# Row sums of one probability tile in four on PoolE in a dilated-attention block

## The chip, the core and the metric

The kernel runs on one core of a Trainium2 chip. The core has a matrix engine (TensorE, PE in the profile, with its weight loads shown apart as PEld), VectorE (DVE), ScalarE (ACT), PoolE (POOL, also GpSimd) and SyncE (SP), which here only issues DMA transfers. Each engine takes its instructions in order, and they wait for each other through semaphores. The metric is the device time of one execution in microseconds, median of several runs.

## The reference

One decoder block on x of 2048 positions by 1024 features, float32. Only the attention matters here:

```python
DILATION_GROUPS = ((128, 1), (512, 4), (2048, 16))   # (window, dilation), 8 heads of 64 in each group
...
s = jnp.einsum('brnqhd,brnkhd->brnhqk', qb, kw) * (Dh ** -0.5)
s = jnp.where(valid[None, None, :, None], s, NEG_INF)      # a causal band, 128 queries by 256 keys
m = jnp.max(s, axis=-1, keepdims=True)
p = jnp.exp(s - m)
l = jnp.sum(p, axis=-1, keepdims=True)
o = jnp.einsum('brnhqk,brnkhd->brnqhd', p, vw)
...
wts = jax.nn.softmax(jnp.stack(lses, axis=0), axis=0)      # lse = m + log(l): the three groups are mixed by it
attn = jnp.sum(wts[..., None] * jnp.stack(outs, axis=0), axis=0)
```

Before it stands one input projection (queries, keys, values, gates), beside it a gated recurrence over positions (its result is `h` below, its output projection `yb`), and behind it the output projections and a layer norm. The row sum `l` is what the change computes in another way.

## The kernel before

The kernel has four stages. **A**, to about 1445 us, is the input projection with the rotary embedding and the recurrence; its results go to scratch tensors in DRAM. **B**, attention, runs to about 1645. **C** is the `yb` products, 32 jobs of 24 matmuls, in whose shadow the three attention groups are combined (`weigh`, `spread`, `combine`). **D** is the remaining projections and the norm.

Stage B is a loop over 48 rounds `i`. Four rounds (`q` = 0 to 3) make a unit `u`, which is one pair of heads of one group; units take the groups in the order 0, 2, 1, and again, for four pairs of heads. A round has four blocks `j` of 128 queries and two heads `h`, so eight score tiles. A score tile has 256 keys, or 128 where there is no block before it: `first(i, j)` is then 128. That holds for all of group 2, for all blocks of the first round of a unit of group 1, and for block 0 in the first round of a unit of group 0. I call such tiles and rounds narrow.

The work of a round is written out by hand and spread over three rounds, so that the engines run side by side:

- `scores(i)`: 24 matmuls into two PSUM tiles for each half round (tag `s`).
- `peak(i, j, h)` on VectorE: adds the mask, writes the tile to SBUF as `p` and takes the row extreme into `sta`. The tile `p` of a block comes from a pool of eight buffers, four of which are used in a round.
- `expo(i, j, h)` on ScalarE, in place on `p`: the Exp, with the row sum as accumulator output into `sta`. In the profile this is two instructions, ACTIVATE and ACTIVATION_READ_ACCUMULATOR (L1023).
- `turn(i-1, w)` on TensorE: transposes the `p` tiles of half a round into PSUM.
- `bring(i-1 or i-2, w, k, engine)`: copies these to SBUF (`ptb`), on VectorE (L1049) or ScalarE (L1047). In each round VectorE has two of the four copies for good; a third, `bring(i-2, 1, 0)`, is VectorE's if `light` is true and ScalarE's if not; the fourth, `bring(i-1, 0, 0)`, is VectorE's if `more` is true.
- `values(i-2)` on TensorE, and `leave(i-3)` on VectorE: the product with V, and its copy out of PSUM.

`leave` also queues the stores of the round (`o_scr`), and for the last pair of heads the store of the statistics `sta` to `st_scr`; they are issued on SP a round later. Stage C reads them back (`load_stats`).

Queries, keys and values of unit u + 2 are loaded from round 4u on (`unit_parts`, `loads`, two pieces a round). The keys of a unit come in two halves, `k_part(0)` and `k_part(1)`; each is cut into two pieces of 512 columns, and each piece is split into a rounded part and its remainder (`split`, lines L809 and L811: a cast and a subtraction). For the first unit ScalarE and VectorE do that, for the others PoolE. `later(lag, fn)` puts a function on a list; `run(late)`, at the start of a round, issues what has become due. From round 40 on the weights `wl` of stage C (`prep_wl`) and the first block of `h` (`load_h`) are loaded, and PoolE splits them too, two rounds later (L1100, L1103): two pieces of weights or of `h` in each of the rounds 42 to 47, and two pairs of weights after the loop.

Of the kernel before, what the change touches and what calls it, by code (L numbers as in the profile page):

```python
# [8 lines left out]
F32 = mybir.dt.float32  # L9
F32R = mybir.dt.float32r  # L10
AF = mybir.ActivationFunctionType
ALU = mybir.AluOpType
# [3 lines left out]
P = 128  # L16
# [4 lines left out]
CH = 512  # L21
# [10 lines left out]
def hybrid_block_kernel(ctx: ExitStack, tc: tile.TileContext, a: dict, out: bass.AP):  # L32
    nc = tc.nc
    sp, act, dve, pool, pe = nc.sync, nc.scalar, nc.vector, nc.gpsimd, nc.tensor

    def flat(t):
        return t.bitcast(F32)
# [24 lines left out]
    cst = ctx.enter_context(tc.tile_pool(name="cst", bufs=1))  # L62
# [15 lines left out]
    act.dma_start(lr, a["lru_vec"])  # L78
    brh = cst.tile([P, 2, 8], F32, name="brh")
    HALF = (slice(0, 64), slice(64, P))  # L80
    gr_free = [cst.tile([P, P], F32, name=f"gr{j}") for j in range(2)]
    sp2 = cst.tile([P, 8], F32, name="sp2")


# [2 lines left out]
    def big(slot, shape, dt, name):  # L87
        return (Y if slot[0] == "Y" else Z if slot[0] == "Z" else X).tile(shape, dt, name=name, tag=slot)
# [5 lines left out]
    def later(lag, fn):  # L94
        late.append((now["n"] + lag, fn))
# [4 lines left out]
    def run(queue):  # L100
        due = [x for x in queue if x[0] <= now["n"]]
        queue[:] = [x for x in queue if x[0] > now["n"]]
        for _, fn in due:
            fn()
# [443 lines left out]
    light = [("v", FT_V + 2 * j, FT_V + 2 * j + 1) for j in range(6)]  # L548
# [157 lines left out]
    for s, pl in enumerate(plan):  # L706
        if pl[4] == "ug" and not (pl[0] and pl[1][1][0] - FT_U in put_off):
            at(base[s] + 1, lambda i=pl[1][1][0] - FT_U: fetch_gr(i))
        if pl[0] and pl[4] == "ug":
            i = pl[1][1][0] - FT_U  # L710
# [38 lines left out]
    def bring(t, b, c):  # L749

        at(t - 3, lambda: [keep_raw(b, c, kk) for kk in K4])
        at(t, lambda: [one_block(b, kk) for kk in K4])
# [36 lines left out]
    def unit(u):  # L789

        return (0, 2, 1)[u % 3], u // 3

    def unit_parts(u):

        qs, ks = USLOT[u % 3]
        g, hp = unit(u)
        q = {n: qk_scr[n, 4 * g + hp] for n in ("qh", "ql", "k")}
        units[u] = [None, None]

        def k_part(j):  # L800
            cols = slice(j * S // 2, (j + 1) * S // 2)

            def split(t):
                K = units[u][1]
                if u == 0:
                    act.activation(K[:, 0, t], flat(K[:, 1, t]), AF.Copy)
                    eng = dve
                else:
                    pool.tensor_copy(K[:, 0, t], flat(K[:, 1, t]))  # L809
                    eng = pool  # L810
                eng.tensor_tensor(out=K[:, 1, t], in0=flat(K[:, 1, t]), in1=flat(K[:, 0, t]), op=ALU.subtract)  # L811

            def fn():
                if j == 0:
                    units[u][1] = big(ks, [P, 2, S], F32R, f"B{u}")
                sp.dma_start(flat(units[u][1][:, 1, cols]), q["k"][:, cols])
                for i in range(2):
                    c0 = (2 * j + i) * CH
                    later(3 + i if u < 2 else 1, lambda c0=c0: split(slice(c0, c0 + CH)))
            return fn  # L820

        def q_part(i, n):
            def fn():
                if i == 0:
                    units[u][0] = big(qs, [P, 2, S], F32R, f"A{u}")
                sp.dma_start(flat(units[u][0][:, i]), q[n])
            return fn

        return [k_part(0), k_part(1), q_part(0, "qh"), q_part(1, "ql")]
# [3 lines left out]
    def v_parts(g, j):  # L833
        src = v_scr[g][j]

        def part(i):
            def fn():
                if i == 0:
                    VT[g, j] = big(VSLOT[g, j], [P, 16, 256], F32, f"V{g}{j}")
                V = VT[g, j]  # L840
                if g == 0:
                    sp.dma_start(V[:, 4 * i:4 * i + 4], src[i * CH:(i + 1) * CH].rearrange("(n p) f -> p n f", p=P))
                elif g == 1:
                    sp.dma_start(V[:, 4 * i:4 * i + 4], src[i * CH:(i + 1) * CH].rearrange("(j r) f -> j r f", r=4))
                else:
                    sp.dma_start(V[:, 4 * i:4 * i + 4], src.rearrange("(i r) f -> i r f", r=16)[:, 4 * i:4 * i + 4])
            return fn

        return [part(i) for i in range(4)]
# [74 lines left out]
    first, second, third, firstv = unit_parts(0), unit_parts(1), unit_parts(2), v_parts(0, 0)  # L924
# [20 lines left out]
    n = len(where)  # L945
# [16 lines left out]
    at_p = stB.enter_context(tc.tile_pool(name="at_p", bufs=2, reuse_waits="tile"))  # L962
# [3 lines left out]
    def prev(g, n):  # L966
        if g == 0:
            return n - 1 if n >= 1 else None
        if g == 1:
            return n - 4 if n >= 4 else None  # L970
        return None

    st = {}

    sta, stg, ot = {}, {}, {}

    def first(i, j):
        u, q = divmod(i, 4)
        g, _ = unit(u)
        return 0 if prev(g, 4 * q + j) is not None else P  # L980
# [29 lines left out]
    def peak(i, j, h):  # L1010
        u, q = divmod(i, 4)
        lo = first(i, j)
        if h == 0:
            st["p", i, j] = p_p.tile([P, 2, 256], F32, tag="p", name=f"p{i}{j}")
        dve.tensor_tensor_reduce(out=st["p", i, j][:, h, lo:256], in0=st["s", i, j // 2][h][:, j % 2, lo:256],  # L1015
                                 in1=mask[:, lo:256], scale=1.0, scalar=3e38, op0=ALU.add, op1=ALU.min,
                                 accum_out=sta[u][:, 4 * q + j, h:h + 1])

    def expo(i, j, h):
        u, q = divmod(i, 4)  # L1020
        p = st["p", i, j][:, h, first(i, j):256]
        s = sta[u][:, 4 * q + j]
        act.activation(p, p, AF.Exp, scale=-1.0, bias=s[:, h:h + 1], accum_out=s[:, 2 + h:3 + h])  # L1023

    def turn(i, w):
        js = (2 * w, 2 * w + 1)
        pp = [st.pop(("p", i, j)) for j in js]
        tag = "s" if (i, w) == (NG - 1, 1) else "t"
        t = st["t", i, w] = [aps.tile([P, 2, 2, 2, 64], F32, tag=tag, name=f"pt{i}{w}{k}", bufs=4) for k in range(2)]
        for j in js:  # L1030
            for x in range(first(i, j) // P, 2):
                for h in range(2):
                    for k, r in enumerate(HALF):
                        pe.transpose(t[k][:, j % 2, x, h, :], pp[j % 2][r, h, x * P:(x + 1) * P], ident[r, r])  # L1034
# [61 lines left out]
    def split(h, l, eng=dve):  # L1096

        r = flat(l)
        if eng is pool:
            pool.tensor_copy(h, r)  # L1100
        else:
            act.activation(h, r, AF.Copy)
        eng.tensor_tensor(out=l, in0=r, in1=flat(h), op=ALU.subtract)  # L1103
# [17 lines left out]
    NG = 48  # L1121
# [4 lines left out]
    for i in range(NG):  # L1126
        u = i // 4
        turns, copied = i > 0, i > 1
        run(late)
        if i in VORD:  # L1130
            loads += v_parts(*VORD[i])
        if i % 4 == 0 and 1 <= u <= 9:
            loads += unit_parts(u + 2)
        for _ in range(2):
            if loads:
                loads.pop(0)()
        light = copied and (unit((i - 2) // 4)[0] == 2 or i % 3 == 1 or i == 2)
        scores(i)
        if i > 2 and ("o", i - 3) in st:
            leave(i - 3)  # L1140
        if copied:
            bring(i - 2, 1, 1, dve)
            if light:
                bring(i - 2, 1, 0, dve)
        if turns:
            expo(i - 1, 2, 1)
        if copied and not light:
            bring(i - 2, 1, 0, act)
        if turns:
            expo(i - 1, 3, 0)  # L1150
            expo(i - 1, 3, 1)
        peak(i, 0, 0)
        expo(i, 0, 0)
        for j, h in ((0, 1), (1, 0), (1, 1)):
            peak(i, j, h)
        if turns:
            turn(i - 1, 0)
            more = i in (1, NG - 1) or i % 4 == 0 and unit(u)[0] == 2
            bring(i - 1, 0, 0, dve if more else act)
            bring(i - 1, 0, 1, dve)  # L1160
        for j, h in ((0, 1), (1, 0), (1, 1)):
            expo(i, j, h)
        if copied:
            values(i - 2)
            if i == NG - 1:
                leave(i - 2, True)
        peak(i, 2, 0)
        peak(i, 2, 1)
        if turns:
            turn(i - 1, 1)  # L1170
        peak(i, 3, 0)
        peak(i, 3, 1)
        expo(i, 2, 0)
        if i in (40, 41):
            prep_wl(i - 40, 2)
        if 42 <= i < 46:
            load_h(0, 2 * (i - 42), 2)
            load_h(0, 2 * (i - 42) + 1, 2)
        if i in (46, 47):
            prep_wl(i - 44, 2)  # L1180
        now["n"] += 1
# [179 lines left out]
    for n in range(32):  # L1361
        c, f = divmod(n, 8)
# [229 lines left out]
```

## Time and profile before

| | us |
|---|---|
| median of 3 runs (2104.13 to 2104.58) | 2104.32 |
| the profiled execution, its own time | 2103.62 |
| its span, first to last instruction | 2101.9 |
| first and last Exp of attention, L1023 | 1445.7, 1641.7 |
| granted TensorE clock, mean | 0.999 |

A row of a timeline gives start, duration, engine, line, operation, output and inputs, shape and count; where the engine stood idle ahead of it, the idle time and what ended it stand in brackets. Durations of neighbours on one engine can overlap by some hundredths of a microsecond, so a price is read from the distance of two starts. VectorE's rows at L1015 are the peaks, eight in each round, so the first of each eight marks the start of a round: round 0 at 1444.7, round 8 at 1475.9, round 42 at 1618.3.

### The profile page before, as it was taken

The page shows a single profiled execution, that of the slowest core. Times are in us where ns is not written, and L with a number is a line of the kernel's source. Part 1 is how long each engine was busy: PE and PEld are TensorE (multiplying, and loading weights), DVE is VectorE, ACT ScalarE, POOL GpSimd, SP SyncE. Part 2 cuts the span into 40 slices and gives each one's busy share as a digit, 9 for nine tenths or more (in the row PEclk, how much of TensorE's full clock was granted, in tenths as well). Part 3 has the DMA queues.
Part 4 walks back from the last instruction along what each step waited for, and adds up shares of the span by engine and source line. Part 5 has one row for each costly group of instructions (what it writes and reads, how often), then busy time and mean ns, then how long its engine had stood idle before and what let it go on. Part 6 is the DMA issues. An engine that isn't in the chain of part 4 may idle for free.

```text
span 2101.9 us, 35814 instructions
## 1 busy us (share of the span) xinstructions
PE 2086.3 (99%) x12016; PEld 1726.9 (82%) x12016; DVE 1662.7 (79%) x3179; ACT 1116.7 (53%) x2341; POOL 493.1 (23%) x468
## 2 busy tenths in 40 slices
PE   8999999999999999999999999999999999999998
PEld 7888888888888888888888888888999888888887
DVE  8987888889988867787877888877999645576667
ACT  6455456457457565666666775766999411211100
POOL 1111111110111011231221222222545344431120
PEclk9999999999999999999999999999999999999999
DMA  8987997987997967777779778769996788864432
GB/s 271 276 261 225 274 285 216 282 283 235 278 294 242 332 208 204 231 227 220 225 254 278 254 252 266 252 219 374 355 359 236 228 296 281 298 224 160 154 105 71
DMA packets 327160, 524.69 MB, mean 250 GB/s; under 512 B 105536, under 2 KB 135232, under 8 KB 323136
## 3 DMA queue, kind: packets, MB, share of 16 engines
q1 hardware_dynamic: 307088, 489.54, 70.5%
q0 software_dynamic: 12256, 19.42, 5.5%
q10 hardware_dynamic: 7632, 13.44, 1.7%
q8 instruction: 96, 1.57, 0.3%
q14 instruction: 88, 0.72, 0.1%
HBM read 317.14 MB, written 190.45 MB: 241 GB/s over the span
## 4 chain that ended last, share of the span: by engine, by line
PE 91%; DVE 3%; DMA 3%; ACT 2%; issue 1%; SPq 0%; DVEq 0%; ACTq 0%
PE q L622 66%; PE yb L1340 3%; PE yb L1341 3%; PE z L1451 3%; PE yb L1342 3%; PE z L1450 3%; PE z L1452 3%; ACT p L1023 2%; DVE p L1015 2%; PE ya L1419 1%; PE ya L1418 1%; PE ya L1420 1%; PE g L492 1%; PE vtp L358 1%; DMA B<-k_scr 1%; DMA o_scr<-ot 1%
## 5 line engine op out<-in xcount | busy, mean ns | idle before, releaser
L622 PE MATMUL q<-xT,hS 128*128 128x512 f32 x1680 | 521.0, 391 | 0.0
L622 PE MATMUL q<-xT,l 128*128 128x512 f32 x1120 | 436.0, 389 | 0.0
L622 PE MATMUL q<-xB,hA 128*128 128x512 f32 x1248 | 388.9, 393 | 6.0 <-ACT xB L215 6.0
L622 PEld LDWEIGHTS q<-xT,hS 128*128 128x128 f32 x1680 | 312.9, 188 | 69.0 <-issue 5.5
L622 PE MATMUL q<-xB,l 128*128 128x512 f32 x904 | 352.9, 390 | 0.0
L622 PEld LDWEIGHTS q<-xB,hA 128*128 128x128 f32 x1248 | 233.8, 189 | 57.3 <-ACT xB L215 6.0
L622 PEld LDWEIGHTS q<-xT,l 128*128 128x128 f32 x1120 | 210.2, 188 | 44.1
L622 PEld LDWEIGHTS q<-xB,l 128*128 128x128 f32 x904 | 170.3, 188 | 36.0
L245 POOL DMA_DIRECT2D wS<-in_w_in_dram x70 | 61.9, 950 | 491.5 <-DMA wS<-in_w_in_dram 140.0
L622 PE MATMUL q<-xB,hS 128*128 128x512 f32 x560 | 174.0, 392 | 0.0
L1023 ACT ACTIVATE p<-p,sta 128x256 f32<-128x256 f32 (+1 forms) x384 | 172.7, 469 | 1.2 <-PE pt L1034 0.8
L622 PE MATMUL q<-xT,hA 128*128 128x512 f32 x560 | 173.0, 390 | 0.0
L269 ACT ACTIVATE hA<-wA 128x512 fp32r<-128x512 f32 x218 | 134.9, 623 | 54.4 <-DMA wA<-in_w_in_dram 24.9
L269 ACT ACTIVATE hS<-S 128x512 fp32r<-128x512 f32 x175 | 109.0, 623 | 79.3 <-DVE S L227 49.0
L227 POOL TENSOR_TENSOR S<-S,wA 128x512 f32<-128x512 f32 x35 | 45.5, 1301 | 391.8 <-DVE S L227 208.8
L622 PEld LDWEIGHTS q<-xT,hA 128*128 128x128 f32 x560 | 104.7, 188 | 23.0 <-issue 1.5
L622 PEld LDWEIGHTS q<-xB,hS 128*128 128x128 f32 x560 | 104.0, 188 | 22.4 <-issue 1.5
L1015 DVE CUSTOM_DVE_ANT_0 p<-s,mask 128x256 f32<-128x256 f32 (+1 forms) x384 | 116.4, 360 | 0.2 <-PE s L1008 0.2
L1451 PE MATMUL z<-wo,mh 128*128 128x512 f32 (+1 forms) x264 | 101.0, 383 | 0.0
L1452 PE MATMUL z<-wo,ml 128*128 128x512 f32 (+1 forms) x264 | 101.0, 383 | 0.0
L1450 PE MATMUL z<-wo,mh 128*128 128x512 f32 (+1 forms) x264 | 101.0, 383 | 0.0
L227 DVE TENSOR_TENSOR l<-wA,hA 128x512 fp32r<-128x512 f32 x113 | 79.3, 702 | 26.9 <-ACT hA L269 26.6
(204 smaller groups left out, 4257.0 us busy)
## 6 DMA issues: line engine op xcount, KB each, us to landing
wA<-in_w_in_dram SPq DMA_DIRECT2D x253, 256.0 KB, 4.7
wl_scr<-l SPq DMA_DIRECT2D x105, 512.0 KB, 5.2
l<-wl_scr SPq DMA_DIRECT2D x105, 512.0 KB, 4.6
sw<-y SPq DMA_DIRECT2D x384, 64.0 KB, 3.2
wS<-in_w_in_dram SPq DMA_DIRECT2D x70, 256.0 KB, 4.8
wS<-in_w_in_dram POOLq DMA_DIRECT2D x70, 256.0 KB, 6.3
qh_scr<-hi SPq DMA_DIRECT2D x48, 256.0 KB, 5.5
v_scr<-vs SPq DMA_DIRECT2D x48, 256.0 KB, 4.4
```

What stands on the lines that cost most here:

```text
L227: eng.tensor_tensor(out=out, in0=in0, in1=in1, op=op)
L245: pool.dma_start(t, w_part(s, x), accum_op=ALU.add)
L269: act.activation(h, r, AF.Copy)
L622: pe.matmul(bank, w[:, ks], x[:, kk, xx], start=(first and i == 0), stop=(last and i == 11))
L1015: dve.tensor_tensor_reduce(out=st["p", i, j][:, h, lo:256], in0=st["s", i, j // 2][h][:, j % 2, lo:256], in1=mask[:, lo:256], scale=1.0, s ...
L1023: act.activation(p, p, AF.Exp, scale=-1.0, bias=s[:, h:h + 1], accum_out=s[:, 2 + h:3 + h])
L1340: pe.matmul(yb, WL[f][:, 0, k], xx[:, 0], start=(k == 0), stop=False)
L1341: pe.matmul(yb, WL[f][:, 0, k], xx[:, 1], start=False, stop=False)
L1342: pe.matmul(yb, WL[f][:, 1, k], xx[:, 0], start=False, stop=(k == 7))
L1450: pe.matmul(z, mh[:, k], w[:, 0, hs], start=(k == 0), stop=False)
L1451: pe.matmul(z, mh[:, k], w[:, 1, hs], start=False, stop=False)
L1452: pe.matmul(z, ml[:, k], w[:, 0, hs], start=False, stop=(k == 7))
```

## The change

Four edits, all for stage B.

1. `expo` no longer asks for the row sum of block `j` = 0, in neither head. After the second of the two Exps it calls the new `add_up(i)`, which issues PoolE additions: the upper half of the columns onto the lower half, for both heads at once, and again until eight columns are left for each head. These stay in `rest_t`, one place for each of the four rounds of a unit. In the last round of the unit three more additions take all four places down to one column, into the same places of `sta` where the accumulator went before.
2. The scratch tile `grt` holds the sums between: it is the two 128 x 128 tiles `gr0` and `gr1` of stage A, now allocated as one.
3. The key splits that PoolE does for units 2 and later are due 3, 4, 5 and 6 rounds after the load instead of all one round after it.
4. `light` and `more` are true less often. `light` loses the rounds with `i % 3 == 1` outside group 2; `more` loses the first rounds of units of group 2. The copies concerned go from VectorE to ScalarE.

```diff
-    gr_free = [cst.tile([P, P], F32, name=f"gr{j}") for j in range(2)]
+    grt = cst.tile([P, 2, P], F32, name="grt")
+    gr_free = [grt[:, j] for j in range(2)]
...
-                    later(3 + i if u < 2 else 1, lambda c0=c0: split(slice(c0, c0 + CH)))
+                    later(3 + i if u < 2 else 3 + 2 * j + i, lambda c0=c0: split(slice(c0, c0 + CH)))
...
         s = sta[u][:, 4 * q + j]
-        act.activation(p, p, AF.Exp, scale=-1.0, bias=s[:, h:h + 1], accum_out=s[:, 2 + h:3 + h])
+        if j:
+            act.activation(p, p, AF.Exp, scale=-1.0, bias=s[:, h:h + 1], accum_out=s[:, 2 + h:3 + h])
+            return
+        act.activation(p, p, AF.Exp, scale=-1.0, bias=s[:, h:h + 1])
+        if h:
+            add_up(i)
+
+    fold_t = grt
+    rest_t = at_p.tile([P, 4, 2, 8], F32, name="rest_t", bufs=1)
+
+    def add_up(i):
+        u, q = divmod(i, 4)
+        src = st["p", i, 0][:, :, first(i, 0):256]
+        n = (256 - first(i, 0)) // 2
+        while n >= 8:
+            dst = rest_t[:, q] if n == 8 else fold_t[:, :, 0:n]
+            pool.tensor_tensor(out=dst, in0=src[:, :, 0:n], in1=src[:, :, n:2 * n], op=ALU.add)
+            src, n = dst, n // 2
+        if q < 3:
+            return
+        while n > 1:
+            pool.tensor_tensor(out=rest_t[..., 0:n], in0=rest_t[..., 0:n], in1=rest_t[..., n:2 * n], op=ALU.add)
+            n //= 2
+        sums = sta[u].rearrange("p (q j) f -> p q j f", j=4)[:, :, 0, 2:4]
+        pool.tensor_tensor(out=sums, in0=rest_t[..., 0], in1=rest_t[..., 1], op=ALU.add)
...
-        light = copied and (unit((i - 2) // 4)[0] == 2 or i % 3 == 1 or i == 2)
+        light = copied and (unit((i - 2) // 4)[0] == 2 or i == 2)
...
-            more = i in (1, NG - 1) or i % 4 == 0 and unit(u)[0] == 2
+            more = i in (1, NG - 1)
```

## The prediction

> **What bounds the kernel now.** I read the page first, then the busy time by windows over the attention stage, then the timeline of each engine there.
>
> ```profile
> span 2101.9 us, 35814 instructions
> PE 2086.3 (99%) x12016; PEld 1726.9 (82%) x12016; DVE 1662.7 (79%) x3179; ACT 1116.7 (53%) x2341; POOL 493.1 (23%) x468
> 1542.23:1591.89 49.66, 49.40 (x895) 45.09 (x892) 49.66 (x238) 49.40 (x209) 22.24 (x24) 1.00 0.85 320
> 1461.86:1645.51 183.65, 182.18 (x3267) 165.78 (x3264) 182.33 (x871) 180.76 (x767) 103.76 (x112) 1.00 0.83 306
> ```
>
> The columns of a window are its length, then PE, PEld, DVE, ACT and POOL busy. TensorE is busy 99% of the whole kernel, but the diff touches only attention, 48 rounds that end at 1645.5. There PE, DVE and ACT are all full, and POOL is the only engine with room: 103.8 of 183.7 us. The first of the two windows is one period of twelve rounds (24 to 35: four each of groups 0, 1 and 2), 49.66 us long. Busy time double counts overlap between neighbours, so I work with start-to-start distances.
>
> **The change part by part.** *ScalarE.*
>
> ```profile
> 1552.88 0.62 ACT L1047 ACTIVATE ptb<-pt 128x512 f32<-128x512 f32 x1
> 1553.36 0.54 ACT L1023 ACTIVATE p<-p,sta 128x256 f32<-128x256 f32 x1
> 1553.75 0.24 ACT L1023 ACTIVATION_READ_ACCUMULATOR p<-p,sta 128x1 f32 x1
> 1553.85 0.55 ACT L1023 ACTIVATE p<-p,sta 128x256 f32<-128x256 f32 x1
> 1569.42 0.36 ACT L1047 ACTIVATE ptb<-pt 128x256 f32<-128x256 f32 x1
> 1569.68 0.39 ACT L1023 ACTIVATE p<-p,sta 128x128 f32<-128x128 f32 x1
> 1410.88 1.95 ACT L384 ACTIVATE y<-y,bh 128x512 f32<-128x512 f32 x3
> 1412.74 0.61 ACT L269 ACTIVATE hA<-wA 128x512 fp32r<-128x512 f32 x1
> ```
>
> An Exp with a row sum holds ACT 0.49 us: 0.40 for the ACTIVATE and 0.09 for the accumulator read. The change drops the read from two of eight Exps a round, 24 a period: 24 x 0.09 = 2.2 us less. That the ACTIVATE itself stays at 0.40 is my choice; the Tanh without a sum (0.62 us for 512 columns, three in 1.86) speaks for it. Copies come in: per period three wide ones at 0.48 (in rounds 25 and 28 by `light`, in 28 by `more`) and one narrow at 0.26 (round 34), together 1.70. ACT goes from 49.4 to 48.9.
>
> *VectorE* loses those four copies.
>
> ```profile
> 1638.36 1.28 DVE L1049 COPY ptb<-pt 128x512 f32<-128x512 f32 x2
> 1639.56 0.42 DVE L1015 CUSTOM_DVE_ANT_0 p<-s,mask 128x256 f32<-128x256 f32 x1
> ```
>
> Two copies take 1.20, so 0.60 each: at least 1.8 and at most 2.4 a period, from 49.66 to about 47.6. *TensorE* gets nothing and loses nothing:
>
> ```profile
> 1539.93 0.71 PE L1034 MATMUL pt<-ident,p 64*128 64x64 f32 x16
> 1544.50 0.71 PE L1034 MATMUL pt<-ident,p 64*128 64x64 f32 x16
> 1519.21 0.43 PE L1034 MATMUL pt<-ident,p 64*128 64x64 f32 x8
> 1522.24 0.44 PE L1034 MATMUL pt<-ident,p 64*128 64x64 f32 x8
> ```
>
> A full round takes 4.57, a round of group 2 takes 3.03. Six full rounds, one slightly smaller and five narrow ones make about 47. So of these three, ACT is last at 48.9: a gain of 0.75 a period, 3 us over the four periods of the stage. That is all this side can give.
>
> *PoolE* is where the cost lies. The additions have no row of their own, so I build them from the nearest ones.
>
> ```profile
> 1463.54 0.61 POOL L809 CAST B<-B 128x512 fp32r<-128x512 f32 x1 [13.63 <-DMA B<-k_scr]
> 1486.32 0.61 POOL L809 CAST B<-B 128x512 fp32r<-128x512 f32 x1 [1.62 <-DMA B<-k_scr]
> 1492.09 0.61 POOL L809 CAST B<-B 128x512 fp32r<-128x512 f32 x1
> 1688.71 2.67 POOL L1285 TENSOR_TENSOR oc<-oc 128x512 f32<-128x512 f32 x2 [38.19 <-DVE oc L1283]
> 1691.45 1.28 POOL L1286 TENSOR_TENSOR oc<-oc 128x512 f32<-128x512 f32 x1
> 2096.07 0.19 POOL L1478 TENSOR_TENSOR mv<-mv,epst 128x1 f32<-128x1 f32 x1 [17.45 <-DVE mv L1469]
> 2096.34 0.89 POOL L1479 TENSOR_TENSOR mv<-mv 128x1 f32<-128x1 f32 x1
> ```
>
> Three splits of 512 columns lie between 1486.32 and 1492.09: 1.92 each. Two dependent additions of 512 columns take 2.74, so 1.37 each from start to start; a dependent one of a single column takes 0.27. Between them I draw a line: 0.27 + 0.00215 per column. An addition followed by independent work is 0.14 cheaper (1.92 less the cast's 0.69, against 1.37). A full tree has 256, 128, 64, 32 and 16 columns: 0.82 + 0.54 + 0.41 + 0.34 + 0.16 = 2.27 us. A narrow one (group 2, and the first round of the others) starts at 128: 1.45. The last round of four adds 32, 16 and 8 columns: 0.92. Bounds for one addition: below, no dependence gap at all (0.14 us less each); above, the gap between 0.19 at one column and the fixed part that a shallower slope would leave; I let it go to 0.05 more each.
>
> Per period that is 12 x 1.92 + 6 x 2.27 + 6 x 1.45 + 3 x 0.92 = 48.1 us against ACT's 48.9: **PoolE goes from half empty to as full as the rest**, and its queue is in order. Two things hang on it. First, the tile p of eight buffers, four a round, so that VectorE's `peak(i+2, 0, 0)` may write only when the first addition of round i has read p; behind that peak in VectorE's queue stand all other peaks, the copies and the `leave`, so TensorE and ScalarE follow. Second, the splits that were free to run as soon as the data landed now stand in line behind additions that wait for the Exps.
>
> The queue is never empty from round 3 on. There the split of unit 2 waits for its keys, which landed at 1463.54 (row above; neither the load nor its place moves), some 6 us after round 3 began, and from then on PoolE has a backlog that 0.8 us a period doesn't clear. So I add up its work from 1463.54 to the moment when the first addition of round 45 has run, on which the first peak of round 47 waits: 40 key splits, 4 of weights and 4 of h, 48 x 1.92 = 92.2; 19 full trees, 43.0; 23 narrow, 33.3; 11 ends of four, 10.2; and the first addition, 0.7. That is 179.4, so round 47 starts at 1642.9.
>
> ```profile
> 1636.99 0.41 DVE L1015 CUSTOM_DVE_ANT_0 p<-s,mask 128x256 f32<-128x256 f32 x1
> 1645.51 0.50 PE L1340 MATMUL yb<-h,wl 128*128 128x512 f32 x1
> 1646.32 0.40 PE L1340 MATMUL yb<-h,wl 128*128 128x512 f32 x1
> 1647.01 0.39 PE L1340 MATMUL yb<-h,wl 128*128 128x512 f32 x1
> 1633.92 1.30 POOL L1103 TENSOR_TENSOR h<-h 128x512 fp32r<-128x512 f32 x1
> 1647.35 3.97 SPq L1111 DMA_DIRECT2D wl<-wf_scr  x8
> 1658.61 1.29 DVE L1103 TENSOR_TENSOR wl<-wl 128x512 fp32r<-128x512 f32 x2
> 1664.27 1.29 DVE L1103 TENSOR_TENSOR wl<-wl 128x512 fp32r<-128x512 f32 x2 [1.16 <-ACT wl L1102]
> 1672.10 0.56 DVE L1259 TENSOR_TENSOR whl<-wgt,whl 128x384 fp32r<-128x384 f32 x1 [0.67 <-ACT whl L1258]
> ```
>
> Round 47 began at 1637.0 before, so this is +5.9. What follows on VectorE is unchanged, so the first yb product moves from 1645.5 to 1651.4. It needs the last h split seven steps of 0.69 in, at 1656.2; PoolE has it at 1654.4 instead of 1635.2. Covered, with 1.8 to spare. Weights 2 and 3 come at 1661.5 and 1665.4, for products (eight steps, 5.5 each) that start at 1662.3 and 1667.8. Covered.
>
> The **SP queue** is moved too. The statistics of the last unit wait for the sums of round 47, at 1657.6, and behind them stand the loads that were issued from 1647.35; they go out some 13.5 later. Against products 5.9 later that is 7.6 of lost slack. Weight 4's first half was split at 1659.2 for a product at 1667.3 (8.1 of slack), weight 5's at 1664.9 for one at 1672.8 (7.9), the combine weights at 1672.7 for a transpose half-way in the seventh product, 1680.9 (8.2). All just enough; I put 0.3 for it. From there TensorE is full and carries the shift to the end: **+6.2 us**.
>
> The profiled execution took 2103.62, 1.7 beyond its span, and lies 0.70 below the median of 2104.32. The shift is put on the median: 2110.5.
>
> [...]
>
> ```profile
> L227 POOL TENSOR_TENSOR sw<-sw,sin 128x512 f32<-128x512 f32 x48 | 73.9, 1552 | 78.0 <-DMA sw<-y 63.3 <-PE q L622 9.4 <-PE g L492 4.3
> L811 POOL TENSOR_TENSOR B<-B 128x512 fp32r<-128x512 f32 x44 | 56.5, 1285 | 3.5
> ```
>
> The same PoolE form takes 1552 ns in the projections and 1285 in attention, although VectorE is full there; so I use the uncontended price. [...]
>
> **The rivals.**
>
> *ScalarE sets the end, faster or no change.* If a small addition costs 0.04 us less than my line or more (220 of them lie on the chain, so 0.03 each are the 5.9), PoolE never holds a peak late in the stage. Then the gain of up to 3 us stays, less what the late keys cost in rounds 5 to 9, where the first addition of round 3 can't run before 1465.5: 2101 to 2104. For it: only the end points of my line are measured. Against: the gap of a dependent instruction shows at both of them.
>
> *PoolE is dearer still.* At 0.05 more per addition the chain is 11 longer, and the slack of the loads behind the statistics, already used up, adds 1 to 3: 2116 to 2125. For it: trees read two strided rows, and no row shows that.
>
> *The accumulator read is not what costs.* If the ACTIVATE without it takes 0.49 as well, the copies alone remain on ACT: 1.70 a period, 6.8 over the stage where PoolE hides none, so 2111. Against: the Tanh row.
>
> **How the numbers follow.** PoolE's chain as summed, 2106 to 2115: 0.57; ScalarE sets the end: 0.24; PoolE dearer: 0.14; accumulator: 0.05. About 0.2%, 4.2 us, is what a measurement of this kernel tells from no change: slower begins at 2108.5, faster ends at 2100.1. Of the first case two thirds lie beyond 2108.5 (0.38), with the third and fourth 0.56; faster by 4.2 needs more than ScalarE gives, so 0.05 from the second case; 0.39 remains. The range from 2101 to 2117 leaves out 0.07 below and 0.12 above.
>
> **What would show it.** Right: PoolE without idle time from about 1463 to 1665; idle time of VectorE ahead of the first peak of a round, released by PoolE, in rounds 5 to 9 and again from 44 on; L1023 with a quarter of its accumulator reads gone and 0.40 to the next; trees of 2.3 and 1.45 us; the first yb product near 1651. Wrong: PoolE idle in mid-stage, or a tree below 1.8 us; yb products that wait for weights by more than 1 us would show the SP queue as the larger cost.

## The result, and the profile after

The changed kernel takes **2111.2 us** (median of 7 runs, 2109.32 to 2112.85), the kernel before 2104.32 (7 runs, 2104.12 to 2105.0). The ratio is 1.0032, 95% interval 1.002 to 1.0043: slower by 0.3%, beyond what its measurement leaves open. The forecast was 2110.5. The profiled execution of the changed kernel took 2110.21 us, 6.6 more than that of before.

The page of the changed kernel:

```profile
span 2108.4 us, 35977 instructions
PE 2087.2 (99%) x12016; PEld 1725.8 (82%) x12016; DVE 1658.4 (79%) x3164; ACT 1116.0 (53%) x2260; POOL 576.7 (27%) x720
PE 88%; POOL 6%; DMA 2%; ACT 2%; issue 1%; DVE 1%; SPq 0%; DVEq 0%; POOLq 0%; ACTq 0%
```

Of the shares of the whole span only PoolE's moved, from 23% to 27%. The third line tells more: in the chain of work that ended last, PoolE holds 6%. Before, it had no share there, by the same line of the page before:

```profile
PE 91%; DVE 3%; DMA 3%; ACT 2%; issue 1%; SPq 0%; DVEq 0%; ACTq 0%
```

The chain now runs through PoolE's queue in attention.

Busy time by windows of the changed kernel (length, PE, PEld, DVE, ACT, POOL; then the granted clock, the DMA share and GB/s). The first is rounds 24 to 35, which lie at 1543.05 to 1592.22 now; the second is the long window that the prediction shows:

```profile
1543.05:1592.22 49.17, 48.41 (x894) 44.54 (x892) 47.85 (x233) 49.03 (x189) 44.19 (x88) 1.00 0.86 327
1461.86:1645.51 183.65, 176.85 (x3175) 161.70 (x3173) 172.30 (x842) 176.29 (x684) 164.20 (x323) 0.99 0.82 304
```

In mid-stage twelve rounds take 49.17 where they took 49.66, and ScalarE, with 49.03, is the one that is full. That is the gain which the change was able to give: 0.49 a period. In the long window, though, TensorE, VectorE and ScalarE all lost 4 to 10 us of busy time and PoolE went from 103.8 to 164.2. A PoolE row's busy time leaves out the 0.08 us between an addition and the one that needs it, so 164 of 184 with 323 instructions is a full engine; the timeline shows that it never stands idle from the first of these rows to the last:

```profile
1463.13 0.61 POOL L810 CAST B<-B 128x512 fp32r<-128x512 f32 x1 [6.26 <-DMA B<-k_scr]
...
1492.10 0.73 POOL L1040 TENSOR_TENSOR grt<-p 128x256 f32<-128x256 f32 x1
1492.92 1.20 POOL L1040 TENSOR_TENSOR grt<-grt 128x128 f32<-128x128 f32 x3
1494.19 0.22 POOL L1040 TENSOR_TENSOR rest_t<-grt 128x16 f32<-128x16 f32 x1
1494.36 0.61 POOL L810 CAST B<-B 128x512 fp32r<-128x512 f32 x1
...
1641.67 0.73 POOL L1040 TENSOR_TENSOR grt<-p 128x256 f32<-128x256 f32 x1
```

The middle rows are one full tree, 2.26 us from its first start to the next split. The first row is the split of unit 2's keys, the last the first addition of round 45, which ends at 1642.40.

What that holds up, by VectorE's timeline (first peaks of rounds 45, 46 and 47) and by the waits of the changed kernel between 1440 and 1700 (total us, times, longest):

```profile
1630.68 0.42 DVE L1016 CUSTOM_DVE_ANT_0 p<-s,mask 128x256 f32<-128x256 f32 x1 [1.90 <-POOL grt L1040]
...
1636.85 0.42 DVE L1016 CUSTOM_DVE_ANT_0 p<-s,mask 128x256 f32<-128x256 f32 x1 [2.06 <-POOL grt L1040]
...
1642.43 0.42 DVE L1016 CUSTOM_DVE_ANT_0 p<-s,mask 128x256 f32<-128x256 f32 x1 [0.94 <-POOL grt L1040]
```

```profile
DVE gB L1371 <- DMA gB<-mg_scr: 22.5, 2, 20.9
ACT wl L1127 <- DMA wl<-wf_scr: 16.5, 1, 16.5
DVE p L1016 <- POOL grt L1040: 6.8, 6, 2.1
```

Round 47's first peak starts 0.03 us after the addition that frees its buffer, and so do the first peaks of rounds 5 to 10 and 44 to 46. Between these two places PoolE catches up: the buffer that round 17 needs is free 2.24 us ahead of its peak, that of round 29 3.37 ahead, that of round 41 4.47 ahead. This lead, about 1.1 a period, is used up by round 44, when the splits for stage C have joined the queue. The first two rows of the waits are the other place of loss; before they were shorter, in the same view of the kernel before:

```profile
DVE gB L1346 <- DMA gB<-mg_scr: 11.7, 1, 11.7
ACT wl L1102 <- DMA wl<-wf_scr: 7.3, 1, 7.3
```

They lead into stage C, whose start lies so in the timeline of the changed kernel (SyncE's queue, VectorE, TensorE):

```profile
1650.70 0.50 PE L1365 MATMUL yb<-h,wl 128*128 128x512 f32 x1
...
1657.11 0.58 SPq L1117 DMA_DIRECT2D st_scr<-sta  x1
1661.83 3.97 SPq L1136 DMA_DIRECT2D wl<-wf_scr  x8
...
1672.44 0.69 DVE L1371 SCALAR_TENSOR_TENSOR gB<-gB,yb 128x512 f32<-128x512 f32 x1 [20.93 <-DMA gB<-mg_scr]
1673.27 0.47 PE L1365 MATMUL yb<-h,wl 128*128 128x512 f32 x1 [0.50 <-DVE gB L1371]
1690.70 0.39 PE L1365 MATMUL yb<-h,wl 128*128 128x512 f32 x1
```

The first product is 5.2 later than before (1645.51). The statistics wait for the last sums and go out at 1657.11; the weight loads behind them at 1661.83 instead of 1647.35. The eighth job starts at 1690.70, 6.5 later than before (1684.18). So stage B gives 5.2 and the first jobs of stage C another 1.3; their sum is the 6.5 between the two spans.

### The profile page after: what moved, and what is told of

The parts are those of the page before. It is cut to its first block, busy times and chain, and to the rows that moved or that the text cites. A ratio compares the mean times of both kernels' runs of the same rounds, so it can differ in the third digit from the quotient of the medians.

```text
span 2108.4 us, 35977 instructions
## 1 busy us (share of the span) xinstructions
PE 2087.2 (99%) x12016; PEld 1725.8 (82%) x12016; DVE 1658.4 (79%) x3164; ACT 1116.0 (53%) x2260; POOL 576.7 (27%) x720
## 4 chain that ended last, share of the span: by engine, by line
PE 88%; POOL 6%; DMA 2%; ACT 2%; issue 1%; DVE 1%; SPq 0%; DVEq 0%; POOLq 0%; ACTq 0%
PE q L623 65%; PE z L1475 3%; PE z L1477 3%; PE z L1476 3%; PE yb L1365 2%; PE yb L1367 2%; PE yb L1366 2%; POOL grt L1040 2%; POOL B L812 2%; PE ya L1443 1%; PE ya L1445 1%; PE ya L1444 1%; PE g L493 1%; PE vtp L359 1%; ACT p L1025 1%
## 5 line engine op out<-in xcount | busy, mean ns | idle before, releaser
L228 POOL TENSOR_TENSOR S<-S,wA 128x512 f32<-128x512 f32 x35 | 45.6, 1303 | 391.3 <-DVE S L228 244.9
L1025 ACT ACTIVATE p<-p,sta 128x256 f32<-128x256 f32 (+1 forms) x288 | 131.3, 475 | 0.2 <-DVE sta L1016 0.2
L1365 PE MATMUL yb<-h,wl 128*128 128x512 f32 x256 | 100.5, 393 | 0.5 <-DVE gB L1371 0.5
```

Source lines behind the costliest of these rows:

```text
L228: eng.tensor_tensor(out=out, in0=in0, in1=in1, op=op)
L1365: pe.matmul(yb, WL[f][:, 0, k], xx[:, 0], start=(k == 0), stop=False)
```

## The experiments

All times are medians, beside the kernel before on the same chip: 2104.28 (26 runs) for the first four, 2104.19 (25) for the next four, 2104.25 (21) for the last two. The table is worked out from each kernel's timeline: rounds by the first peak of each, then the distance from round 47's first peak to the first yb product.

| | round 0 to 12 | 12 to 24 | 24 to 36 | 0 to 47 | 47 to yb | median |
|---|---|---|---|---|---|---|
| before | 47.90 | 49.64 | 49.66 | 192.30 | 8.52 | 2104.3 |
| changed kernel | 49.39 | 48.91 | 49.17 | 197.68 | 8.27 | 2111.2 |
| e1, copies as before | 53.69 | 49.65 | 49.65 | 202.22 | 8.45 | 2111.2 |
| e2, first addition only | 47.82 | 49.18 | 49.18 | 190.80 | 8.40 | 2102.5 |
| e3, no trees from 40 on | 49.43 | 48.92 | 49.17 | 192.25 | 9.40 | 2105.4 |
| e4, no trees | 48.09 | 51.00 | 51.00 | 196.54 | 9.40 | 2110.1 |
| e5, trees in 8 to 39 | 47.57 | 49.16 | 49.17 | 190.55 | 8.49 | 2102.6 |
| e6, e5 with `more` | 47.56 | 49.15 | 49.17 | 190.50 | 8.50 | 2102.9 |
| e7, statistics later | 49.22 | 48.91 | 49.15 | 197.15 | 8.27 | 2109.1 |
| e8, splits early | 63.14 | 50.91 | 49.70 | 211.15 | 8.27 | 2124.9 |
| e9, e5 with `light` | 47.56 | 48.86 | 48.85 | 189.90 | 8.49 | 2103.0 |
| e10, both | 47.55 | 48.87 | 48.85 | 189.92 | 8.50 | 2101.9 |

**e1: the copies as before.**

```diff
-        light = copied and (unit((i - 2) // 4)[0] == 2 or i == 2)
+        light = copied and (unit((i - 2) // 4)[0] == 2 or i % 3 == 1 or i == 2)
...
-            more = i in (1, NG - 1)
+            more = i in (1, NG - 1) or i % 4 == 0 and unit(u)[0] == 2
```

> The change with the copies given back: light and more as before, trees and spread splits kept. Theory (PoolE's in-order queue sets the end): its work between the landing of unit 2's keys and round 45 is the same, so the first peak of round 47 stays near 1642.4 and the time within 1.5 us of the changed kernel, 2109.5 to 2112.5. Rival (the copies that ScalarE took are the cost): the time falls back to 2102 to 2105.

Measured 2111.16 (2110.31 to 2114.44, 5 runs), ratio 1.0035 [1.0023, 1.0047]. The copies do not make the change slow. What was expected of round 47 did not come: in the profiled execution, the longest of the five, its first peak lies at 1646.44 and not near 1642.4, as 4.3 were lost in the first twelve rounds (see the last section). That trace shows one thing more. PoolE stood idle in mid-stage, for the last time ahead of the tree of round 39, and VectorE's first peaks of rounds 45 and 46 still waited 1.23 and 1.72 for PoolE:

```profile
1613.34 0.73 POOL L1040 TENSOR_TENSOR grt<-p 128x256 f32<-128x256 f32 x1 [0.50 <-ACT p L1027]
```

So the late waits come without a backlog from the start of the stage. The window of rounds 24 to 35 of e1 also says what bounded the kernel before:

```profile
1547.56:1597.21 49.65, 49.13 (x896) 45.09 (x892) 49.65 (x238) 47.94 (x185) 43.09 (x88) 1.00 0.85 320
```

ScalarE is down to 47.94, and the period stays at 49.65 with VectorE busy for all of it. Relief of ScalarE alone buys nothing; the copies must move too.

**e2: only the first addition of each tree.**

```diff
-        while n >= 8:
-            dst = rest_t[:, q] if n == 8 else fold_t[:, :, 0:n]
-            pool.tensor_tensor(out=dst, in0=src[:, :, 0:n], in1=src[:, :, n:2 * n], op=ALU.add)
-            src, n = dst, n // 2
+        pool.tensor_tensor(out=fold_t[:, :, 0:n], in0=src[:, :, 0:n], in1=src[:, :, n:2 * n], op=ALU.add)
...
-        pool.tensor_tensor(out=sums, in0=rest_t[..., 0], in1=rest_t[..., 1], op=ALU.add)
+        some = fold_t[:, 0, 0:8].rearrange("p (q f) -> p q f", f=2)
+        pool.tensor_tensor(out=sums, in0=some, in1=some, op=ALU.add)
```

> Of each tree only the first addition is issued, and one short one in the last round of a unit: the row sums of block 0 are left out, the wait of the peaks on PoolE stays. Theory: PoolE has idle time, no peak waits for it, and what is left is the gain of ScalarE and VectorE alone, 0.6 to 0.75 us per twelve rounds: 2101 to 2102.5. Rival (any wait on PoolE costs, however short its work): 2107 or more. Rival (ScalarE gains nothing without the accumulator read): 2104 or more.

This kernel leaves out the row sums of block 0. Measured 2102.47 (11 runs, 2101.57 to 2105.7), ratio 0.9993 [0.9985, 1.0002]. The waits of e2 between 1440 and 1700:

```profile
POOL grt L1038 <- ACT p L1027: 50.8, 32, 2.7
DVE p L1016 <- POOL grt L1038: 1.3, 2, 1.1
```

Now PoolE waits for ScalarE, 32 times, and no peak late in the stage waits for PoolE. The ratios of e2 and the changed kernel lie 0.0039 apart, 8.2 us: that is what the rest of the trees costs, delayed statistics included.

**e3: accumulators again from round 40 on.**

```diff
-        if j:
+        if j or i >= 40:
```

> From round 40 on block 0 gets its row sum by ScalarE's accumulator again, trees before that. Theory (the loss arises where the trees stand in line with the splits of weights and h, rounds 42 to 47, and behind them the statistics): rounds 44 to 47 no longer wait for PoolE, the shift of -0.9 that round 40 has stays, the statistics of the last unit go out at once: 2102.5 to 2104.5. Rival (the backlog from the late keys of round 3 is what counts): at most half of the 7 us comes back, 2107 or more.

Measured 2105.37 (11 runs, 2103.66 to 2106.56), ratio 1.0005 [0.9997, 1.0014]: nearly all of the loss is gone, so it is paid in the last eight rounds, where the splits for stage C join PoolE's queue. It is 0.9 above the upper end of what was expected. The table shows where: rounds 0 to 40 are those of the changed kernel, but from round 47 to the first yb product 9.40 us pass instead of 8.27, as in e4. Both keep accumulators in these rounds together with the extra copies on ScalarE; that this is the cause of the 9.40 was not tested by itself.

**e4: accumulators everywhere, copies moved.**

```diff
-        if j:
-            act.activation(p, p, AF.Exp, scale=-1.0, bias=s[:, h:h + 1], accum_out=s[:, 2 + h:3 + h])
-            return
-        act.activation(p, p, AF.Exp, scale=-1.0, bias=s[:, h:h + 1])
-        if h:
-            add_up(i)
+        act.activation(p, p, AF.Exp, scale=-1.0, bias=s[:, h:h + 1], accum_out=s[:, 2 + h:3 + h])
```

> No trees: all row sums by the accumulator; copies and spread splits as changed. Theory: ScalarE is last, 49.4 + 1.7 = 51.1 us per twelve rounds against 49.66, 1.4 a period and 5 to 6 over the stage: 2108 to 2111. Rival (ScalarE had room for the copies): 2102 to 2105.

Measured 2110.14 (9 runs: eight from 2109.19 to 2111.21, and one of 4218.09, which the ratio leaves out), ratio 1.0027 [1.0017, 1.0038]. The window of rounds 24 to 35 of e4:

```profile
1544.70:1595.70 51.00, 48.71 (x892) 44.57 (x891) 48.67 (x233) 51.00 (x215) 22.37 (x25) 1.00 0.84 313
```

ScalarE is full, 51.00 of 51.00; the prediction's sum for this, 49.4 plus 1.70 of copies, is 51.1. With e2's 49.18 beside it, dropping the reads is worth 1.82 a period; in ScalarE's busy time it is 1.96 (e2 has 49.04), where the prediction had summed 2.2.

**e5: trees in rounds 8 to 39 only, copies as before elsewhere.**

```diff
-        if j:
+        if j or not 8 <= i < 40:
...
-        light = copied and (unit((i - 2) // 4)[0] == 2 or i == 2)
+        light = copied and (unit((i - 2) // 4)[0] == 2 or i % 3 == 1 and not 8 <= i < 40 or i == 2)
...
-            more = i in (1, NG - 1)
+            more = i in (1, NG - 1) or i in (4, 40)
```

> Trees only in rounds 8 to 39, units 2 to 9; before and after these the accumulator, and light and more by their old rules there. Theory (the trees cost nothing where PoolE has only key splits beside them; the loss stands at both ends): no stall in rounds 5 to 9 and none from 44 on, and of the gain that the shortened trees showed between rounds 8 and 40 (2.2 us) all but half a microsecond stays: 2101.5 to 2103. Rival (trees and key splits together are already more than PoolE holds): stalls in mid-stage, 2105 or more.

Measured 2102.57 (11 runs, 2102.06 to 2106.5), ratio 0.9995 [0.9986, 1.0004]. It keeps the gain of mid-stage and pays neither early nor late: 190.55 from round 0 to 47 against 192.30. Its period, though, is 49.17, not the 48.9 that the sum gave. In the timeline of e5, TensorE's product of round 14 stands in round 16, the first of a unit of group 2, behind a ScalarE copy:

```profile
1511.34 1.97 PE L1089 MATMUL o<-ptb,V 128*64 128x128 f32 x32 [0.23 <-ACT ptb L1072]
1513.36 0.69 DVE L1100 COPY ot<-o 128x512 f32<-128x512 f32 x1 [0.63 <-PE o L1089]
```

**e6: e5 with the copy of `more` back on VectorE.**

```diff
-            more = i in (1, NG - 1) or i in (4, 40)
+            more = i in (1, NG - 1) or i % 4 == 0 and unit(u)[0] == 2
```

> As the trees in rounds 8 to 39, and the more copy in the first round of a unit of group 2 goes back to VectorE. Theory: in the changed kernel ScalarE brings that copy about 0.6 us later than VectorE did, TensorE's products and VectorE's leave wait for it, so each of rounds 16 and 28 gives back up to 0.7 us: 0.5 to 1.5 us below the kernel without this edit, 2100.5 to 2102. Rival (VectorE becomes last again): no difference or slower.

Measured 2102.85 (11 runs, 2101.62 to 2104.51), ratio 0.9994 [0.9985, 1.0003]: a miss. The table has no difference to e5, and e6's product of round 14 still waits for ScalarE's copy, 0.24. VectorE's idle 0.63 behind it is gone, and the period is the same, so VectorE's wait did not set it. It was the wrong one of the two copies.

**e7: the last unit's statistics behind the weight loads.**

```diff
-            later(1, lambda: sp.dma_start(dst[cs].rearrange(form, q=P), src[:, 4 * q:4 * q + 4]))
+            fn = lambda: sp.dma_start(dst[cs].rearrange(form, q=P), src[:, 4 * q:4 * q + 4])
+            if u == 11:
+                stats_last.append(fn)
+            else:
+                later(1, fn)
...
+    for fn in stats_last:
+        fn()
```

The loop at the end stands behind the last loads of weights in stage B.

> The changed kernel, with the four statistics stores of the last unit issued on SP behind the loads of weights 4 to 7 instead of ahead of them. Theory: the wait of SP on PoolE's last sums costs only what stage C lost beyond the shift of its start (1.3 us from the first to the seventh yb product), so 2109 to 2110.7. Rival (the SP queue, through which the changed kernel's chain of waits runs, is the larger cost): 2108 or less.

Measured 2109.13 (9 runs, 2108.73 to 2110.08), ratio 1.0025 [1.0015, 1.0034], 2.1 below the changed kernel by the medians. SyncE's queue in e7's timeline:

```profile
1652.81 3.98 SPq L1142 DMA_DIRECT2D wl<-wf_scr  x8
1657.97 2.62 SPq L1119 DMA_DIRECT2D st_scr<-sta  x4
```

The loads go out 1.2 us after the first yb product (1651.60) and not 11.1 after it, and stage C, from the first yb product to VectorE's last `gB` row, takes 187.89 as against 189.20 in the changed kernel and 187.87 before. So the statistics cost the 1.3 that the profile of the changed kernel showed; of the rest, 0.5 lies in stage B by the table, and what is left is within the two intervals.

**e8: the key splits one round after the load, as before.**

```diff
-                    later(3 + i if u < 2 else 3 + 2 * j + i, lambda c0=c0: split(slice(c0, c0 + CH)))
+                    later(3 + i if u < 2 else 1, lambda c0=c0: split(slice(c0, c0 + CH)))
```

> The changed kernel with the key splits due one round after the load again, all four together. Theory (PoolE's queue is in order, so a split that waits for its keys holds the tree behind it): keys land about 10 us after their issue, the four splits take 7.7, and the tree of the next round comes some 17.7 us after the unit began where a peak waits for it after 13.5; 4 to 5 us in each of ten units, 2135 to 2165. Rival (spreading the splits does nothing): 2109 to 2113.

Measured 2124.9 (4 runs, 2124.66 to 2125.69), ratio 1.0101 [1.0085, 1.0116]. The direction held, the size did not. Nearly all of it falls in the first twelve rounds, 63.14 instead of 49.39. A row of e8's PoolE timeline and one of its VectorE timeline:

```profile
1463.24 0.61 POOL L810 CAST B<-B 128x512 fp32r<-128x512 f32 x1 [10.99 <-DMA B<-k_scr]
1471.61 0.29 DVE L1016 CUSTOM_DVE_ANT_0 p<-s,mask 128x128 f32<-128x128 f32 x1 [9.04 <-POOL grt L1040]
```

The first splits stand in PoolE's queue ahead of a tree, and wait for keys. Not all of the loss is this wait. Windows of e8:

```profile
1464.00:1468.00 4.00, 0.99 (x24) 0.68 (x18) 0.00 (x0) 0.37 (x2) 3.84 (x5) 0.96 1.00 411
1468.00:1472.00 4.00, 0.03 (x1) 0.03 (x1) 0.39 (x3) 0.05 (x1) 3.84 (x5) 0.50 1.02 406
1472.00:1480.00 8.00, 7.37 (x64) 6.82 (x64) 4.96 (x30) 6.33 (x28) 6.56 (x20) 0.50 1.04 421
1480.00:1488.00 8.00, 6.97 (x115) 6.28 (x113) 4.77 (x23) 3.39 (x15) 7.63 (x10) 0.92 0.55 196
```

TensorE was busy for 1.02 of the 8 us up to 1472, and in the 8 us behind them, with 7.37 busy again, its granted clock was 0.50; from 1480 to 1488 its mean was 0.92. The next twelve rounds lose 2.0, the twelve behind them 0.5: only one later split, at 1546.52, still waits for its keys, and 0.9 at that. The spread of the splits is thus needed, once, at the start.

**e9 and e10: e5 with `light` back on VectorE in rounds 16 and 28; e10 has `more` of e6 as well.**

```diff
-        light = copied and (unit((i - 2) // 4)[0] == 2 or i % 3 == 1 and not 8 <= i < 40 or i == 2)
+        light = copied and (unit((i - 2) // 4)[0] == 2 or i % 3 == 1 and not 8 <= i < 40 or i in (2, 16, 28))
```

> As e5_mid_trees, but VectorE takes the `light` copy back in rounds 16 and 28, the first rounds of two units of group 2. Theory: in e5's and the changed kernel's trace the product of the last full round stood waiting there for ScalarE's late copy, and some 0.7 us of the gain was lost in each such unit; with the copy on VectorE again about 0.4 us each comes back, so 2101.3 to 2102.3 against 2102.6 of e5, and the first peak of round 47 lies 2 us or more earlier than before, where it lay 1.4 to 1.5 earlier in e5. Rival: TensorE had caught up by the next round and the loss is ScalarE's sum of work in those rounds: 2102.3 to 2103, round 47 no earlier than in e5.

> As e9_mid_light, and the `more` copy of the same two rounds back on VectorE as well, so that ScalarE keeps only two extra copies in twelve rounds and gives back all that it gained in the narrow rounds. Theory: 2101 to 2102.3, the same as e9 within 0.5 us, since e6 showed that this copy alone changes nothing. Rival (VectorE, with both copies, becomes the last in those rounds): 2102.5 to 2104.

Measured 2102.95 for e9 (11 runs, 2101.18 to 2105.33), ratio 0.9994 [0.9985, 1.0003], and 2101.86 for e10 (11 runs, 2100.99 to 2103.34), ratio 0.9988 [0.9979, 0.9997]. e9's median misses its expectation by 0.65 and sits in the rival's range. Its profiled execution agrees with the theory: period 48.85 instead of 49.17, rounds 0 to 47 in 189.90, 2.4 less than before. e10's does the same, 189.92. Two traces that agree to 0.02 and two medians 1.1 apart mean that medians cannot part e5, e6, e9 and e10; what the `light` copy brings, 0.3 a period, is shown by the traces alone. In e9's TensorE timeline the product of round 14 no longer waits:

```profile
1511.52 1.97 PE L1089 MATMUL o<-ptb,V 128*64 128x128 f32 x32
```

The window of rounds 24 to 35 of e10:

```profile
1541.11:1589.96 48.85, 48.30 (x896) 44.48 (x894) 48.78 (x236) 48.37 (x187) 43.43 (x89) 1.00 0.87 330
```

VectorE (48.78), ScalarE (48.37) and TensorE (48.30) are within half a microsecond of each other. e10 is the one version whose interval lies wholly below the kernel before, by 0.12% at its centre. As e9, with the same trace, does not reach that, and as e10 is the best of several versions alike, this is weak evidence that it is faster.

## Why the prediction held, step by step

*PoolE's chain* carried the forecast and was right almost to the tenth. Full tree 2.25 (2.27 predicted), narrow tree 1.44 (1.45), end of four 0.91 (0.92). From unit 2's first split to the end of round 45's first addition 179.3 (179.4). No row of before gives the 2115 at which this case ended; the seven runs of the changed kernel reach 2112.85. Round 47 began at 1642.43 (1642.9), because the keys landed 0.4 earlier than in the profile of before. The line drawn between two distant rows holds at every size in between: additions of 256, 128, 64 and 32 columns take 0.82, 0.54, 0.40 and 0.33 from start to start (0.82, 0.54, 0.41 and 0.34 predicted). Both of its end points held the gap of a dependent instruction, 0.08 us in the changed kernel's rows. e3, and e1's trace, show that the end of the stage is where it decides, and e2 that without the rest of the trees no late peak waits.

*The PoolE price of 1285 ns* was the right one of the two rows: the key subtractions still average 1285 ns, by PoolE's groups of the changed kernel between 1463 and 1646:

```profile
L812 POOL TENSOR_TENSOR B<-B 128x512 fp32r<-128x512 f32 x40 | 51.4, 1285 | 3.2
```

In the projections of the changed kernel PoolE's rows of 128 x 512 have two means, 1567 ns (48 of `sw<-sw,sin`, L228) and 1303 (35 of `S<-S,wA`, L228). What makes the first dearer, and so that 1285 is a price without contention, was not shown.

*The accumulator read is what costs.* In the changed kernel's ScalarE timeline:

```profile
1554.09 0.53 ACT L1027 ACTIVATE p<-p,sta 128x256 f32<-128x256 f32 x1
1554.49 0.52 ACT L1025 ACTIVATE p<-p,sta 128x256 f32<-128x256 f32 x1
1554.89 0.21 ACT L1025 ACTIVATION_READ_ACCUMULATOR p<-p,sta 128x1 f32 x1
1554.98 0.52 ACT L1025 ACTIVATE p<-p,sta 128x256 f32<-128x256 f32 x1
```

An Exp without a sum (first row) holds ScalarE 0.40 until the next, one with a sum 0.49, as the prediction chose from the Tanh. That rival is out.

*ScalarE last at 48.9, a gain of 0.75 a period:* the engine was right (49.03 of 49.17), the gain was 0.49. The step that fell short is the sum by engines alone: it left out that the copies moved in rounds 16, 28 and 40 come late in ScalarE's order, so that the product behind one of them waits. e6 shows that it is not the `more` copy, and the trace of e9 that it is the `light` one. Each of the two takes one wide copy off ScalarE in rounds 24 to 35, whose busy time falls from 49.03 (e5) to 48.73 and 48.70, and only e9's shortens the period (48.85 for 49.17). So it is the wait and not ScalarE's sum of work. By the first peaks of the changed kernel, rounds 24, 27 and 33 got shorter (4.88 to 4.28, 5.15 to 4.55, 4.35 to 4.01), rounds 28 and 29, where these copies come, longer (4.08 to 4.43, 3.31 to 4.01), and the others stayed, the narrow rounds 30 to 32 at 3.28 among them. A sum over the whole period does not show this. The early rounds cost more than they gain: 49.39 for the first twelve instead of 47.90.

*ScalarE sets the end* was a rival at 2101 to 2104, and e2 gives its time, 2102.5, when PoolE is relieved. It failed only because PoolE's backlog was real.

*The shift after round 47* was to be 5.9 and was 5.2: 0.4 from the keys, 0.25 from a shorter tail. The last `h` split was in time, as predicted.

*The SyncE queue* was mis-sized: the loads went out 14.5 later (13.5 predicted), the slack of 8 was indeed used up, and the term of 0.3 measured 1.3, by the distance of two rows and by e7's trace. The two errors nearly cancel, 5.2 + 1.3 against 5.9 + 0.3. That the total came so close is luck in this part: each term was off by 0.7 to 1.0.

Of the signs, PoolE without idle time, the idle times of VectorE from round 44 on, the shape of the trees and the first yb product (1650.7 for 1651) came as written. Of the early idle times that PoolE ends, the profile has two, 1.44 ahead of round 6 and 0.17 ahead of round 10; the 0.83 ahead of round 5 is put down to TensorE, and in rounds 7 to 9 VectorE keeps PoolE's pace without a visible pause. The sign set for a larger SyncE cost, yb products waiting for weights by more than 1 us, came only in part: the waits were for `gB` and for weights, spread over several jobs, none above 1 us by itself.

## What to carry to other kernels

An engine that is half idle on average can still become the bound when work is moved to it, as PoolE did here (busy 103.8 of the 183.65 us before, 164.2 after, and without a wait from 1463.13 to 1642.40): take the last moment at which it is certain to be idle, add up its in-order work from there to the first instruction that someone else waits for, and compare that with the time at which it is needed. Here the same trees went with a gain of 2.4 us in rounds 8 to 40 (132.65 instead of 135.01) and a loss of 6.3 in rounds 40 to 47 (32.41 instead of 26.11), where the next stage's splits shared the queue. So the place of such work matters as well as its amount: less work everywhere (e2) and the same work kept away from the end (e3) each took the loss away. When a result comes later, look also at what is queued behind its store, not only at who reads it: here the weight loads went out 14.5 later, and the first jobs of stage C lost 1.3.

## What had not been expected

**The granted TensorE clock was 0.50 for some microseconds after a short stall, in some executions.** Windows of the changed kernel, three of 4 us and a shorter one. In the first, TensorE waits 1.96 us in round 45 for a copy held up behind that round's late peak:

```profile
1628.00:1632.00 4.00, 2.04 (x36) 1.66 (x32) 2.10 (x10) 1.86 (x9) 3.61 (x8) 1.00 0.43 163
1632.00:1636.00 4.00, 3.63 (x46) 3.33 (x46) 2.79 (x13) 3.55 (x14) 3.68 (x7) 0.71 0.20 82
1636.00:1640.00 4.00, 3.45 (x50) 2.81 (x48) 3.15 (x16) 2.68 (x9) 3.69 (x8) 0.87 0.92 248
1633.70:1637.00 3.30, 3.30 (x34) 3.08 (x36) 1.24 (x5) 1.85 (x9) 3.14 (x5) 0.50 0.54 199
```

The 0.71 and the 0.87 are means over a step: from 1633.7 to 1637.0 the granted clock is 0.50, and 1.00 before and behind that. In e1's profiled execution, the longest of its five runs, the same happened early, after an idle time of 1.31:

```profile
1472.00:1476.00 4.00, 3.76 (x47) 3.62 (x49) 4.00 (x26) 3.92 (x18) 3.69 (x8) 0.68 1.04 416
1476.00:1480.00 4.00, 4.00 (x44) 3.67 (x40) 2.80 (x18) 2.62 (x13) 3.60 (x8) 0.50 1.02 420
1480.00:1484.00 4.00, 4.00 (x46) 3.55 (x46) 2.66 (x14) 2.98 (x14) 3.45 (x10) 0.54 1.03 414
```

By the means of 0.68 and 0.54, and if the clock fell and rose in one step each, it is 0.50 from about 1473.4 to about 1483.7. In the middle window TensorE is busy all the time, with 44 instructions where the changed kernel has 68, and the first twelve rounds took 53.69 instead of 49.39. The changed kernel in its own profile kept 1.00 in these windows. In e8 the clock fell within the idle time: TensorE's last busy time ended near 1465.0 (0.99 from 1464), and the mean of 0.96 up to 1468 puts a single step to 0.50 at about 1467.7. So a stall of PoolE's making may cost more than its own length: in e1, 1.31 of idle time stood ahead of some 10 us at 0.50, and the twelve rounds took 4.3 longer. What decides whether the clock falls with a short stall is not shown, and how much of the change's loss, or of e1's 4.3, is of this kind was not measured by itself.
